# Output weights scaled by the gate, summed and split beside attention, and read back from DRAM by the output stage

## The chip, the cores and the metric

One NeuronCore of a Trainium2 chip. It has five engines with a queue of instructions each: TensorE (PE, matmuls, with a queue PEld for loading its stationary operand), VectorE (DVE), ScalarE (ACT), GpSimd (POOL) and SyncE (SP). Here SP does nothing but issue DMAs; ACT issues some too. DMAs move data between DRAM and SBUF, the on-chip memory; matmuls write to PSUM, eight banks of 128x512 float32. Every engine works through its queue in order and waits on semaphores. The metric is device time in microseconds (us) of one execution, the median of several runs.

## The reference, cut to what matters

One layer of a hybrid backbone over 2048 latent tokens of width 1024 (and 256 context tokens). One input projection feeds two token mixers: a gated DeltaNet, which gives `ya` (2048x512), and windowed attention, which gives `yb` (2048x512). Then

```python
def _merge(ya, yb, ga, gb, w_proj_a, w_proj_b, w_out):
    y = jax.nn.sigmoid(ga) * (ya @ w_proj_a) + jax.nn.sigmoid(gb) * (yb @ w_proj_b)
    return y @ w_out
...
x = x + gate[:, None] * _merge(ya, yb, ga, gb, w_proj_a, w_proj_b, w_out)
```

`gate` is a row of 1024 numbers that depends on the conditioning alone; `w_out` is 1024x1024. So the last stage is `x + gate * (y @ w_out)`, and the gate scales columns of `w_out`.

## The kernel before

Float32 products are made of reduced-precision ones: each operand is split into a high half (a cast, on ACT or POOL) and a low half (operand minus high half, on DVE or POOL), and a product is three matmuls per 128 rows of depth: high x high, high x low, low x high.

The parts that stand near the change, in order:

- **Attention** (`attention`, L943): 32 units, one for each of 16 blocks of 128 tokens and 2 key/value heads, in the token groups 1, 2, 0, 3 of 512 tokens. A unit's scores are made two units ahead (L978 masks, takes the minimum and reads PSUM; L980 exponentials; L988 scales on POOL), then `weighted` transposes them on PE, splits them (L1004 ACT, L1006 DVE) and multiplies by the values; L1014 on POOL multiplies by a gate and L1015 stores `yb`.
- **Gates** (`gates`, L892) fill PE between the units: columns 15 to 23 of the gate projections. Their weights are split at L243 and L244.
- **Projection** (`project`, L1280): for each token group, eight slices m of 128 channels of y, each the sum of two products, each scaled by a gate column from DRAM (L1304, L1309). For the groups 1, 2 and 0 they fill PE between attention's later units; group 3 comes after attention. y is stored to the scratch tensors `ysp` (L1310). The last two sums of group 3 are made late, within the output stage (`late_sum`, L1313). The projection's pool `proj` is opened at L1338, and its first loads of raw weights are at L1341.
- **Outputs** (from L1369): y is cut into 8 units of 256 tokens, each a 2x2 of quarters A11, A12, A21, A22 (128 tokens by 512 channels); `w_out` into quarters B11 to B22 of 512x512. Strassen's method in Winograd's form gives seven products per unit instead of eight: P1 = A11 B11, P2 = A12 B21, P3 = S4 B22, P7 = S3 T3, P6 = S2 T2, P5 = S1 T1, P4 = A22 T4, where S1 to S4 are sums of quarters of y (functions `s1` to `s4`), and T1 to T4 sums of quarters of `w_out`. One product is 12 matmuls of 128x512 (`product`, L1533 to L1541). `seq` is their order: for units 0 and 1 by turns, then unit by unit. `his(k)` casts the high half of product k's y operand on ACT five products ahead, `los(k)` makes the low half four products ahead (DVE, for P4 POOL). `outputs(k)` collects the finished product: sums of products in `held`, multiplication by the gate (`gbc`, the gate row on all partitions), addition of x (L1492) and the store (L1493), which also asks for the x tile four outputs on.

In the output stage the weight work is done on the spot: `load_w` brings the raw quarters on ACT's DMA queue, behind the last split of y for group 3; high halves are cast at L1438 to L1447, L1570, L1580 and L1585, low halves made in `split_lo` (L1411) on DVE and, for B22 and T3, on POOL; the sums T3, T2, T1, T4 are made in place at L1444, L1446, L1578 and L1583, between the products.

**What sets the order.** A planner (the tile framework) orders each engine's instructions by their place in the program and its own estimate of times: an instruction that is ready goes ahead of later ones, and later ones fill what is idle. `issue_after(i)` queues instructions behind i on its engine. Within `manual_schedule` the named engines keep the written order; in the output stage these are DVE, ACT, POOL and PE. SP's order is the planner's. SBUF is handed out in stacks from two sides; a tile that takes the bytes of an earlier one waits until that one was used for the last time.

Of the kernel before, what the change touches and what calls it, by code (L numbers as in the profile page):

```python
# [11 lines left out]
ALU = mybir.AluOpType  # L12
# [28 lines left out]
def _hybrid(ctx, tc, nc, V, S, G, T, ins, out, dbg, upto):  # L41
# [67 lines left out]
    ysp = many("ysp", 4, [128, KT, 512])  # L109
# [833 lines left out]
    def attention(pool, big, blocks, cc):  # L943
# [336 lines left out]
    def project(pool, wp, gi, yy=None, first=-99, late=()):  # L1280
# [3 lines left out]
        for m in range(KT):  # L1284
# [25 lines left out]
            dma(ysp[gi][:, m], us[0])  # L1310
        return left

    def late_sum(gi, m, us):  # L1313
        def run():
# [8 lines left out]
            dma(ysp[gi][:, m], ts[0])  # L1323
# [11 lines left out]
    attention(al, ar, [4 * gi + j for gi in (1, 2, 0, 3) for j in range(4)], att_consts(al))  # L1335
    gates(list(range(BESIDE, 22)), (1, 0))
# [37 lines left out]
    with tc.tile_pool(name="p4h", bufs=1, side="right", reuse_waits="tile") as hr, \  # L1374
# [9 lines left out]
        home = {"B11": er, "B21": er, "B22": el, "B12": el}  # L1384

        B = {nm: po.tile([128, 4, 512], F32, name=nm, tag=nm) for nm, po in home.items()}
        hi = {nm: BH(po, nm + "h") for nm, po in home.items()}
        hi["T3"] = hi["B12"]
        lo = {"B11": BH(er, "B11l")}
        A, Y = {}, {}  # L1390

        def load_w(nm):
            i, j = int(nm[1]) - 1, int(nm[2]) - 1
            adma(B[nm], ins["w_out"][0, i * 512:i * 512 + 512, j * 512:j * 512 + 512].rearrange("(k p) c -> p k c", p=128))

        def load_quad(u, nm):
            gi, o = units[u]
            if nm == "A2":
                t = p4.tile([128, 8, 128], F32, name="yA2", tag=f"yA2{u % 2}")
                adma(t, ysp[gi][:, :, o + 128:o + 256])  # L1400
                Y[u, "A21"], Y[u, "A22"] = t[:, 0:4], t[:, 4:8]
                return
            c = int(nm[2]) - 1
            po = {(0, "A11"): el, (0, "A12"): er, (1, "A11"): er}.get((u % 2, nm), p4)
# [3 lines left out]
        def split_lo(nm, eng, src=None, place=None):  # L1408
            if place:
                lo[nm] = home[place].tile([128, 4, 512], F32R, name=nm + "l", tag=place)  # L1410
            eng.tensor_tensor(lo[nm], B[src or nm], f32(hi[nm]), op=ALU.subtract)  # L1411
# [14 lines left out]

        with tc.high_priority(tc.cur_priority - p_last), \
                tc.manual_schedule(engines={EN.DVE, EN.Activation, EN.Pool}):
            with tc.issue_after(last["yh", 3].ins):
                load_w("B11")  # L1430
                load_quad(0, "A11")
                load_quad(1, "A11")
                load_w("B22")
                load_w("B12")
                load_w("B21")
                load_quad(0, "A12")
            with tc.issue_after(last["yh", 3].ins), tc.issue_after(last["yl", 3].ins):
                S.copy(hi["B11"], B["B11"])  # L1438
                split_lo("B11", V)
                for k in range(2):  # L1440
                    his(k)
                    los(k)
                S.copy(hi["B22"], B["B22"])
                V.tensor_tensor(B["B12"], B["B22"], B["B12"], op=ALU.subtract)  # L1444
                S.copy(hi["B21"], B["B21"])
                V.tensor_tensor(B["B11"], B["B12"], B["B11"], op=ALU.add)  # L1446
                S.copy(hi["T3"], B["B12"])  # L1447


        lo["B21"] = BH(hr, "B21l")  # L1450
        for k in range(2, NP):
            pair(k)
        for nm in ("B22", "T3"):
            lo[nm] = BH(hr, nm + "l")
        for nm in ("T2", "T1", "T4"):
            hi[nm] = BH(hr, nm + "h")
# [206 lines left out]
```

## Time and profile before

| | us |
|---|---|
| three runs, median (lowest, highest) | 1975.54 (1973.47, 1983.3) |
| the profiled execution: time / span | 1977.22 / 1975.5 |
| PE, DVE, ACT, POOL busy | 1902.6, 1512.4, 815.6, 701.3 |
| attention's first and last score (L978) | 1339.3, 1724.6 |
| first and last matmul of the outputs start | 1801.2, 1967.5 |

In the profile's rows L12 is line 12 of the kernel. A row of a timeline gives start, duration, engine, line, operation, output<-input, count, and in brackets how long the engine had stood idle and what released it. A row of waits gives who waited for whom: us in total, times, longest. A row of groups gives line, operation, count, then busy us in total and mean ns of one, then the idle time before them. PEclk, or the granted clock, is the share of full speed at which PE was allowed to run.

### The profile page before, as it was taken

The numbers are of one execution on the slowest core, as the hardware profiler recorded it, in microseconds if no ns is written. First come the engines' busy times: TensorE is split into PE (matmuls) and PEld (weight loads), VectorE is DVE, ScalarE is ACT, GpSimd is POOL, SyncE is SP. The second block draws the span as 40 slices with busy tenths as digits, with TensorE's granted clock in tenths as the row PEclk, the third lists the DMA queues.
The fourth block names the chain that finished last, engine by engine and source line by source line (L and its number), as shares of the span: only waits on it lengthen the run. The fifth ranks groups of instructions, "written<-read, shape, count | busy, mean of one in ns | idle before, by whom it ended". The sixth has DMA issues, their size and how long they took to land. (4 is left out here: it accounts for less than half of the span.)

```text
span 1975.5 us, 32093 instructions
## 1 busy us (share of the span) xinstructions
PE 1902.6 (96%) x10931; PEld 1596.3 (81%) x10931; DVE 1512.4 (77%) x2873; ACT 815.6 (41%) x2011; POOL 701.3 (35%) x772
## 2 busy tenths in 40 slices
PE   6899999989999899999999999999999999999998
PEld 3888888788998787887888888888878887877786
DVE  7888766678776899999778776535787868757888
ACT  6865545544443322211122233324765646532321
POOL 2652111235543201104222334323555443422675
PEclk9999999999999999999999999999999999999999
DMA  7453226765546633537887777765455645355453
GB/s 267 161 154 93 87 89 161 190 166 166 152 146 169 178 108 115 151 96 208 230 251 219 224 227 228 197 182 188 136 182 178 195 150 173 113 190 175 144 171 134
DMA packets 387640, 333.13 MB, mean 169 GB/s; under 512 B 83928, under 2 KB 307472, under 8 KB 386836
## 3 DMA queue, kind: packets, MB, share of 16 engines
q1 hardware_dynamic: 352132, 288.58, 50.4%
q10 hardware_dynamic: 35344, 42.49, 6.2%
q8 instruction: 87, 1.43, 0.3%
q14 instruction: 77, 0.63, 0.1%
HBM read 220.28 MB, written 109.13 MB: 167 GB/s over the span
## 5 line engine op out<-in xcount | busy, mean ns | idle before, releaser
L586 PE MATMUL rps<-hh,wh 128*128 128x512 f32 x768 | 308.5, 402 | 6.5 <-DVE rt L880 5.4
L588 PE MATMUL rps<-hh,wl 128*128 128x512 f32 x768 | 307.7, 401 | 0.2 <-DVE wl L244 0.2
L587 PE MATMUL rps<-hl,wh 128*128 128x512 f32 x768 | 306.3, 399 | 0.0
L625 DVE SCALAR_TENSOR_TENSOR cacc<-y,cw,cacc 128x512 f32<-128x512 f32 (+1 forms) x224 | 163.5, 752 | 23.3 <-ACT cacc L623 21.0
L586 PEld LDWEIGHTS rps<-hh,wh 128*128 128x128 f32 x768 | 144.9, 189 | 41.8 <-DVE rt L880 6.3
L588 PE MATMUL lps<-hh,wl 128*128 128x512 f32 (+1 forms) x448 | 171.6, 383 | 1.7 <-DVE wl L244 1.7
L586 PE MATMUL lps<-hh,wh 128*128 128x512 f32 (+1 forms) x448 | 172.0, 384 | 0.8 <-POOL wh L243 0.6
L588 PEld LDWEIGHTS rps<-hh,wl 128*128 128x128 f32 x768 | 144.8, 188 | 32.6 <-DVE wl L244 0.3
L587 PEld LDWEIGHTS rps<-hl,wh 128*128 128x128 f32 x768 | 144.8, 189 | 32.5
L587 PE MATMUL lps<-hl,wh 128*128 128x512 f32 (+1 forms) x448 | 171.0, 382 | 0.0
L1006 DVE TENSOR_TENSOR pl<-pt,ph 128x512 fp32r<-128x512 f32 x156 | 105.6, 686 | 42.3 <-ACT ph L1004 41.4
L1004 ACT CAST ph<-pt 128x512 fp32r<-128x512 f32 x156 | 90.8, 585 | 107.8 <-PE pt L1002 72.8
L878 ACT ACTIVATE rt<-rps 128x512 f32<-128x512 f32 x96 | 57.2, 596 | 181.5 <-PE rps L588 157.9
L978 DVE CUSTOM_DVE_ANT_0 pr<-sc,band,sk 128x640 f32<-128x640 f32 (+1 forms) x128 | 106.7, 862 | 19.8 <-PE sc L974 12.1
L988 POOL TENSOR_SCALAR pr<-pr,sm 128x640 f32<-128x640 f32 (+1 forms) x128 | 101.4, 813 | 54.7 <-DVE sm L986 39.9
L809 DVE TENSOR_TENSOR btmp<-N 128x62 f32<-128x62 f32 (+30 forms) x124 | 117.4, 946 | 3.1
L811 DVE TENSOR_TENSOR N<-N,btmp 128x62 f32<-128x62 f32 (+30 forms) x124 | 116.1, 936 | 3.0
L980 ACT ACTIVATE pr<-pr,sm 128x640 f32<-128x640 f32 (+1 forms) x128 | 104.1, 815 | 24.1 <-DVE sm L978 24.1
L1293 PE MATMUL pps<-yh,wph 128*128 128x512 f32 x256 | 105.7, 415 | 2.4 <-DVE tb L1304 2.1
L244 DVE TENSOR_TENSOR wl<-wr,wh 128x512 fp32r<-128x512 f32 x120 | 91.6, 775 | 20.2 <-POOL wh L243 17.9
L243 POOL TENSOR_SCALAR wh<-wr 128x512 fp32r<-128x512 f32 x72 | 49.5, 700 | 156.4 <-PE lps L587 85.2
L1295 PE MATMUL pps<-yh,wpl 128*128 128x512 f32 x256 | 101.6, 398 | 0.9 <-POOL wpl L1255 0.9
(382 smaller groups left out, 5028.2 us busy)
## 6 DMA issues: line engine op xcount, KB each, us to landing
wr<-in_w_in_dram SPq DMA_DIRECT2D x120, 256.0 KB
kw<-Ksp SPq DMA_DIRECT2D x28, 384.0 KB
x<-vsp SPq DMA_DIRECT2D x36, 256.0 KB
k<-ksp SPq DMA_DIRECT2D x34, 256.0 KB
kT<-kTsp SPq DMA_DIRECT2D x34, 256.0 KB
wm<-in_w_mod_dram SPq DMA_DIRECT2D x16, 512.0 KB
xt<-in_x_dram SPq DMA_DIRECT2D x16, 512.0 KB
dtl<-Dsp SPq DMA_DIRECT2D x32, 256.0 KB
```

The costliest lines, as they stand in the source:

```text
L586: T.matmul(ps, lhsT=wh[:, k], rhs=xh[:, k], start=k == 0, stop=False)
L587: T.matmul(ps, lhsT=wh[:, k], rhs=xl[:, k], start=False, stop=False)
L588: T.matmul(ps, lhsT=wl[:, k], rhs=xh[:, k], start=False, stop=k == kt - 1)
L625: V.scalar_tensor_tensor(a, y[:, t:t + n], cw[:, m, t:t + 1], a, op0=ALU.mult, op1=ALU.add)
L809: V.tensor_tensor(tv, A[:, m + 1:, m].unsqueeze(2).to_broadcast([h1 + n, r, m]), A[:, m, 0:m].unsqueeze(1).to_broadcast([h1 + n, r, m]), o ...
L811: V.tensor_tensor(A[:, m + 1:, 0:m], A[:, m + 1:, 0:m], tv, op=ALU.add)
L978: V.tensor_tensor_reduce(s_, ps[:, o:768], band[:, b0:b0 + W + 256], -0.125, sk[:, 1, hd:hd + 1], ALU.add, ALU.min, sm[:, h, 1:2])
L980: S.activation(s_, s_, AF.Exp, scale=-1.0, bias=sm[:, h, 1:2], accum_out=sm[:, h, 2:3])
L988: G.tensor_scalar(p[:, h, :W + 256], p[:, h, :W + 256], sm[:, h, 3:4], 1.0, op0=ALU.mult, op1=ALU.mult)
L1006: V.tensor_tensor(pl, pt, f32(ph), op=ALU.subtract)
L1293: T.matmul(ps, lhsT=wh[:, k, ms], rhs=hs[k], start=k == 0, stop=False)
L1295: T.matmul(ps, lhsT=wl[:, k, ms], rhs=hs[k], start=False, stop=k == 3)
```

## The change

1. A generator `out_weights` runs beside attention: one step after each unit, 25 steps. For each of four slices of 128 rows it loads that slice of the four quarters of `w_out`, multiplies them by the gate row (`gbc`, POOL), makes T3, T2, T1 and T4 in place (POOL), casts the high half of each of the seven (ACT), makes the low half (DVE), and stores both to the scratch tensors `wsp` in DRAM. Its pool `wout` is closed behind attention and the gates; the pool `proj` opens at the same place of the left stack.
2. In the output stage `load_w` loads finished high and low halves: B11, B21, B22, T3 on ACT's queue with the first quarters of y, T2, T1 and T4 on SP's queue, between the first x tiles. All casts, splits and sums of weights are gone from there, and s3 and s2 of units 0 and 1 stand ahead of the products.
3. As the weights hold the gate, outputs need no multiplication: `gather` adds a product, or a sum in `held`, straight into the x tile; `store` adds the last product to it from PSUM and stores it. P1 is added on POOL, P3 on DVE, the three sums behind P6 on POOL (for the last unit on DVE). Eight x tiles instead of four are kept.
4. `ysp` is laid out as [4, 128, 8, 128], one block for each 128 tokens, so that a quarter of y is contiguous per partition (2 KB, or 4 KB for A21 and A22 together) and a store is cut into runs of 512 bytes.

```diff
-    ysp = many("ysp", 4, [128, KT, 512])
+    ysp = many("ysp", 4, [4, 128, KT, 128])
+    wsp = {nm: [dscr(f"w{nm}{x}", [128, 4, 512]) for x in "hl"] for nm in ("B11", "B21", "B22", "T3", "T2", "T1", "T4")}
...
+    def out_weights(pool):
+        gbc = pool.tile([128, D], F32, name="gbc")
+        dma(gbc, gsp.to_broadcast([128, D]))
+        b = {}
+        def load(k):
+            for nm in ("B22", "B12", "B11", "B21"):
+                i, j = int(nm[1]) - 1, int(nm[2]) - 1
+                b[nm] = pool.tile([128, 512], F32, name=nm)
+                dma(b[nm], ins["w_out"][0, i * 512 + k * 128:i * 512 + k * 128 + 128, j * 512:j * 512 + 512])
+        def gated(nm):
+            j = int(nm[2]) - 1
+            G.tensor_tensor(b[nm], b[nm], gbc[:, j * 512:j * 512 + 512], op=ALU.mult)
+        def put(k, nm, t):
+            h = pool.tile([128, 512], F32R, name="woh", bufs=2)
+            l = pool.tile([128, 512], F32R, name="wol", bufs=2)
+            S.copy(h, t)
+            V.tensor_tensor(l, t, f32(h), op=ALU.subtract)
+            for dst, p in zip(wsp[nm], (h, l)):
+                dma(dst[:, k], f32(p))
+        load(0)
+        yield
+        for k in range(4):
+            gated("B22")
+            gated("B12")
+            yield
+            put(k, "B22", b["B22"])
+            G.tensor_tensor(b["B12"], b["B22"], b["B12"], op=ALU.subtract)
+            gated("B11")
+            yield
+            put(k, "T3", b["B12"])
+            put(k, "B11", b["B11"])
+            G.tensor_tensor(b["B11"], b["B12"], b["B11"], op=ALU.add)
+            yield
+            gated("B21")
+            put(k, "T2", b["B11"])
+            G.tensor_tensor(b["B22"], b["B22"], b["B11"], op=ALU.subtract)
+            yield
+            put(k, "T1", b["B22"])
+            put(k, "B21", b["B21"])
+            G.tensor_tensor(b["B21"], b["B21"], b["B11"], op=ALU.subtract)
+            yield
+            put(k, "T4", b["B21"])
+            if k < 3:
+                load(k + 1)
+            yield
...
             weighted(n, kv, qs[n], pr.pop(i))
+            next(beside, None)
...
-            dma(ysp[gi][:, m], us[0])
+            dma(ysp[gi][:, :, m].rearrange("o p c -> p o c"), us[0].rearrange("p (o c) -> p o c", c=128))
...
-        def load_w(nm):
-            i, j = int(nm[1]) - 1, int(nm[2]) - 1
-            adma(B[nm], ins["w_out"][0, i * 512:i * 512 + 512, j * 512:j * 512 + 512].rearrange("(k p) c -> p k c", p=128))
+        def load_w(nm, queue=adma):
+            for t, x, src in zip((hi, lo), "hl", wsp[nm]):
+                t[nm] = BH(home.get(nm, hr), nm + x)
+                queue(f32(t[nm]), src)
...
-            adma(Y[u, nm], ysp[gi][:, c * 4:c * 4 + 4, o:o + 128])
+            adma(Y[u, nm], ysp[gi][o // 128][:, c * 4:c * 4 + 4])
...
-        def store(u, q, t, eng):
-            xr, dst, gate, j = X.pop((u, q))
-            eng.tensor_tensor(t, t, gate, op=ALU.mult)
-            (V if u == 7 else G).tensor_tensor(xr, t, xr, op=ALU.add)
+        def gather(eng, u, q, t):
+            xr = X[u, q][0]
+            eng.tensor_tensor(xr, t, xr, op=ALU.add)
+        def store(u, q, ps):
+            gather(V, u, q, ps)
+            xr, dst, j = X[u, q]
             dma(dst, xr)
-            load_x(j + 4)
+            load_x(j + 8)
...
             if nm == "P1":
                 S.copy(held[u][:, 0], ps)
+                gather(G, u, "00", held[u][:, 0])
             elif nm == "P2":
-                og = ev.tile([128, 512], F32, name="og", tag="rt")
-                V.tensor_tensor(og, ps, held[u][:, 0], op=ALU.add)
...
+                store(u, "00", ps)
+            elif nm == "P3":
+                gather(V, u, "01", ps)
             elif nm == "P6":
                 V.tensor_tensor(held[u][:, 0], ps, held[u][:, 0], op=ALU.add)
                 V.tensor_tensor(held[u][:, 1], R[u, "P7"], held[u][:, 0], op=ALU.add)
+                gather(gp, u, "11", held[u][:, 1])
+                gather(gp, u, "01", held[u][:, 0])
+                gather(gp, u, "10", held[u][:, 1])
             elif nm == "P5":
-                h2 = wq.tile([128, 2, 512], F32, name="hold2", tag="wl")
-                V.tensor_tensor(h2[:, 0], ps, held[u][:, 0], op=ALU.add)
-                V.tensor_tensor(h2[:, 1], ps, held[u][:, 1], op=ALU.add)
-                V.tensor_tensor(h2[:, 0], R[u, "P3"], h2[:, 0], op=ALU.add)
...
+                store(u, "11", ps)
+                store(u, "01", ps)
             elif nm == "P4":
-                V.tensor_tensor(held[u][:, 1], ps, held[u][:, 1], op=ALU.add)
-                store(u, "10", held[u][:, 1], gp)
+                store(u, "10", ps)
...
+            for j in range(2):
+                load_x(j)
+            load_w("T2", dma)
+            for j in range(2, 8):
+                load_x(j)
+            for nm in ("T1", "T4"):
+                load_w(nm, dma)
```

More of the change, by code (lines that the diff above doesn't have):

```diff
@@ L941, in att_consts, with attention @@
         return kc, vc, sk, band
-    def attention(pool, big, blocks, cc):
+    def out_weights(pool):
[43 more added lines that the diff above has]
+            yield
+    def attention(pool, big, blocks, cc, beside=()):
         kc, vc, sk, band = cc
@@ L1334, in _hybrid @@
     ar = ar_.__enter__()
-    attention(al, ar, [4 * gi + j for gi in (1, 2, 0, 3) for j in range(4)], att_consts(al))
-    gates(list(range(BESIDE, 22)), (1, 0))
+    with tc.tile_pool(name="wout", bufs=1, reuse_waits="tile") as wo:
+        attention(al, ar, [4 * gi + j for gi in (1, 2, 0, 3) for j in range(4)], att_consts(al), out_weights(wo))
+        gates(list(range(BESIDE, 22)), (1, 0))
     wp, last = {}, {}
@@ L1425, in los @@
             (G if nm == "P4" else V).tensor_tensor(A[k][1], Y[u, OPS[nm][0]], f32(A[k][0]), op=ALU.subtract)
[L1427 to L1456, printed above, removed]
         def s3(u, eng):
@@ L1473, in s1 @@
             Y[u, "S1"] = Y[u, "A11"]
-        R, held, early = {}, {}, {}
+        with tc.high_priority(tc.cur_priority - p_last), \
+                tc.manual_schedule(engines={EN.DVE, EN.Activation, EN.Pool}):
+            with tc.issue_after(last["yh", 3].ins):
+                load_w("B11")
+                load_quad(0, "A11")
+                load_quad(1, "A11")
+                load_w("B21")
+                for q in ((0, "A12"), (0, "A2"), (1, "A12"), (1, "A2")):
+                    load_quad(*q)
+                load_w("B22")
+                load_w("T3")
+            with tc.issue_after(last["yh", 3].ins), tc.issue_after(last["yl", 3].ins):
+                for k in range(2):
+                    his(k)
+                    los(k)
+                s3(0, V)
+                s2(0, V)
+                s3(1, V)
+                s2(1, V)
+        for k in range(2, NP):
+            pair(k)
+        R, held = {}, {}
         outs = [(u, q) for u, nm in seq for q in {"P2": ["00"], "P5": ["11", "01"], "P4": ["10"]}.get(nm, [])]
@@ L1540, in product @@
                 T.matmul(ps, lhsT=h[:, j], rhs=wl[:, j], start=False, stop=False)
-                end = T.matmul(ps, lhsT=l[:, j], rhs=wh[:, j], start=False, stop=j == 3)
-            return end
+                T.matmul(ps, lhsT=l[:, j], rhs=wh[:, j], start=False, stop=j == 3)
         with tc.manual_schedule(engines={EN.DVE, EN.Activation, EN.Pool, EN.PE}):
@@ L1546, in _hybrid @@
                 next(j)
-            split_lo("B21", V)
+            for j in range(2):
[5 more added lines that the diff above has]
+                load_w(nm, dma)
             his(2)
-            for q in ((1, "A12"), (0, "A2"), (1, "A2")):
-                load_quad(*q)
-            gbc = p4.tile([128, D], F32, name="gbc")
             los(2)
-            next(sums67[0])
+            s4(0)
             his(3)
             los(3)
-            split_lo("B22", G)
-            split_lo("T3", G, "B12")
-            s3(0, V)
-            s2(0, V)
-            s4(0)
+            next(sums67[0])
             his(4)
+            s4(1)
             for k in range(len(seq) + 1):
@@ L1592, in _hybrid @@
                     load_quad(2, "A2")
-                    for u in range(2):
-                        store(u, "00", *early[u])
                 elif k == 11:
@@ L1610, in _hybrid @@
                 if k < len(seq):
-                    end = product(k)
-                if k == 3:
-                    with tc.issue_after(end.ins):
-                        dma(gbc, gsp.to_broadcast([128, D]))
-                        for j in range(4):
-                            load_x(j)
+                    product(k)
                 if k:
```

54 lines of the change are left out of this document (9 added, 45 removed).

## The prediction

> **What bounds the kernel now.** I read the page's busy times first, then a table of stretches of the span, then the stalls of TensorE in the last stage, then the order of time around them.
>
> ```profile
> PE 1902.6 (96%) x10931; PEld 1596.3 (81%) x10931; DVE 1512.4 (77%) x2873; ACT 815.6 (41%) x2011; POOL 701.3 (35%) x772
> ```
>
> TensorE (PE) is the bound: at most 1975.5 - 1902.6 = 72.9 us of the span are not its matmuls. The change removes no matmul, so it can only win or lose idle PE time. Where that lies (columns: stretch, length, then PE, PEld, DVE, ACT and POOL busy with counts, granted clock, DMA share, GB/s):
>
> ```profile
> 1339.00:1350.00 11.00, 11.00 (x51) 9.07 (x50) 4.97 (x14) 4.17 (x10) 1.25 (x2) 1.00 0.83 269
> 1350.00:1452.00 102.00, 100.94 (x563) 84.97 (x562) 77.54 (x175) 69.87 (x154) 48.72 (x55) 1.00 0.46 142
> 1452.00:1500.00 48.00, 44.70 (x241) 36.68 (x240) 37.48 (x72) 30.80 (x65) 33.33 (x30) 1.00 0.63 198
> 1875.00:1968.00 93.00, 92.88 (x402) 74.94 (x400) 79.59 (x89) 19.29 (x35) 65.44 (x41) 1.00 0.48 156
> ```
>
> Attention begins at 1339. Its first eight units (to 1452) run with PE full, filled by gate columns; then the projections fill it. From 1875 to 1968 the outputs run with PE full too: one product of 12 matmuls takes 12 x 93/402 = 2.78 us there. The idle time of the output stage lies before, in six stretches, and behind it:
>
> ```profile
> 1805.00:1810.00 5.00, 2.38 (x11) 1.63 (x9) 5.00 (x1) 0.00 (x0) 4.87 (x2) 1.00 1.05 349
> 1810.00:1815.00 5.00, 4.52 (x13) 3.57 (x14) 4.65 (x8) 0.62 (x1) 0.00 (x0) 0.66 0.74 209
> 1830.00:1835.00 5.00, 3.44 (x15) 2.51 (x14) 5.00 (x5) 2.82 (x4) 0.00 (x0) 1.00 0.00 0
> 1850.00:1855.00 5.00, 3.98 (x18) 2.94 (x18) 5.00 (x8) 2.35 (x5) 3.68 (x3) 1.00 0.85 243
> 1855.00:1860.00 5.00, 3.39 (x15) 2.47 (x14) 5.00 (x7) 0.00 (x0) 3.68 (x4) 1.00 0.80 259
> 1865.00:1870.00 5.00, 4.28 (x19) 3.16 (x18) 2.59 (x3) 0.02 (x1) 5.00 (x4) 1.00 0.38 125
> ```
>
> The idle PE time adds up to 2.62 + 0.48 + 1.56 + 1.02 + 1.61 + 0.72 = 8.0 us. In 1810 to 1815 the clock was 0.66, which stretched 4.52 busy us by about 4.52 x 0.34 = 1.5 us. What ends these stalls, and why the first is so long (waits of the stage, then DVE and POOL in order of time):
>
> ```profile
> PE P L1541 <- DVE al L1425: 7.3, 4, 3.1
> PE P L1541 <- POOL al L1425: 0.7, 1, 0.7
> PE pps L1293 <- DVE tb L1304: 2.1, 1, 2.1
> ...
> 1798.45 2.29 DVE L1411 TENSOR_TENSOR B21l<-B,B21h 128x2048 fp32r<-128x2048 f32 x1 [1.99 <-PE pps L1294]
> 1800.66 9.76 DVE L1425 TENSOR_TENSOR al<-yA,ah 128x512 fp32r<-128x512 f32 x1
> ...
> 1798.71 6.59 POOL L1411 TENSOR_TENSOR B22l<-B,B22h 128x2048 fp32r<-128x2048 f32 x1 [41.01 <-PE pps L1295]
> 1805.26 4.61 POOL L1411 TENSOR_TENSOR T3l<-B,B12h 128x2048 fp32r<-128x2048 f32 x1
> ```
>
> The first two rows say that all eight us are waits for low halves. The one of 9.76 us ends at 1810.4, just behind POOL's two weight splits (1809.9). So a DVE operation with two SBUF operands stands still while POOL works on SBUF.
>
> **The change, part by part.**
>
> *Output stage, weights.* It loses, on DVE, four sums and five splits of 128x2048 (2.29 us each, 20.6 us), on POOL the two splits of 11.2 us, and on ACT seven big casts; the last of them stand between PE's products. The stall at 1805 loses its cause. So do those at 1830, where DVE is full (5.00 of 5.00) with big sums ahead of the low half, and at 1850 to 1860, where DVE is full with the gate multiplications.
>
> *Output stage, outputs.* Per unit DVE had nine operations on outputs (one for P2, two for P6, three plus two gate multiplications for P5, one for P4) and gets seven; POOL had two multiplications and four additions and gets four. Two new waits: the store of 00 on DVE waits for POOL's addition of P1 into x, and the additions of P5 wait for POOL's three of P6. Queued behind them on DVE are low halves that PE needs three to four products later (8 to 11 us), against three POOL additions of 1.68 us (L1492 below); I put that at 0, at most one POOL operation per unit. I take 7 of the 8 us and the clock's 1.5: **-8.5**; ends 0 (other DVE waits take their place) and -9.5 (all).
>
> *Tail.* After the last matmul:
>
> ```profile
> 1967.48 0.40 PE L1541 MATMUL P<-T4h,al 128*128 128x512 f32 x1
> ...
> 1971.81 0.69 DVE L1527 TENSOR_TENSOR xr<-hold,xr 128x512 f32<-128x512 f32 x1
> 1972.53 0.33 SPq L1528 DMA_DIRECT2D out_dram<-xr  x1
> ```
>
> PE ends at 1967.88, DVE's backlog at 1972.50, the span at 1975.5: 7.6 us. Afterwards one addition from PSUM is left (0.69), 0.1 of hand-over, and the same store (1975.5 - 1972.53 = 2.97): 3.8 us. P5's two additions are done by then, as P4 takes 2.78. **-3.8**; ends -2 (a store queued behind P5's two) and -4.
>
> *Weights come late.* Seven pairs, 14 x 1.05 MB = 14.7 MB, are read where 4.2 MB were. B11, B21, B22, T3 and the first halves of y go on ACT's queue, 10.5 MB, from the time of the first row. T2, T1 and T4 lie where the projection's weights were and can't start before those are read for the last time:
>
> ```profile
> 1764.12 0.39 ACTq L1394 DMA_DIRECT2D B<-in_w_out_dram  x1
> 1798.38 0.62 ACT L1421 CAST ah<-yA 128x512 fp32r<-128x512 f32 x1 [14.20 <-PE pps L1294]
> ...
> L1539 PE MATMUL P<-B11h,ah x32: 387/393/398, 1801.2 to 1950.4; 128*128 128x512 f32 x32
> ...
> DMA packets 3809, 5.25 MB, mean 328 GB/s; under 512 B 122, under 2 KB 1629, under 8 KB 3808
> ```
>
> The second row shows such a start today. From 1798.6 there follow 1.05 MB for the late sums, T2, eight x tiles, T1 and T4, 9.4 MB: at the 349 GB/s of the stretch from 1805, 27 us, so T4 at 1826. The outputs start at 1801.2, and it is needed 12 products later, 1801 + 12 x 2.78 = 1834. The margin of 8 us pays for 3 MB of leftover, new y quarters and stores; the last row is the rate of 1764 to 1780, which also holds the wait for its first bytes. I take **+1.5**, a mid of 0 and the late case below, nearer to 0; the first low half may also wait for the projection's last matmul, 0 to 1 us, within this.
>
> *y quarters.* Stores of y go in runs of 512 B (2 KB before), 32 of 256 KB; loads in runs of 2 or 4 KB (512 B before). The rows give no time by run length. PE waited 2.1 us for the projection's sums in the whole trace (third row of the waits), so I take 0, ends -1 and +2.
>
> *Attention.* Added there: 16 loads and 28 x 2 stores of 256 KB, 32 POOL operations, 28 casts and 28 subtractions of 128x512. Prices (groups of 1339 to 1452, then of the output stage):
>
> ```profile
> L982 DVE TENSOR_TENSOR es<-sm,sk 128x4 f32<-128x4 f32 x11 | 4.1, 371 | 0.0
> L1255 POOL TENSOR_TENSOR wpl<-wpr,wph 128x512 fp32r<-128x512 f32 x4 | 5.1, 1289 | 2.4 <-ACT wph L1254 2.4
> L1274 ACT CAST yh<-yr 128x512 fp32r<-128x512 f32 x4 | 2.3, 612 | 0.0
> L1275 DVE TENSOR_TENSOR yl<-yr,yh 128x512 fp32r<-128x512 f32 x2 | 1.3, 689 | 0.0
> ...
> L1492 POOL TENSOR_TENSOR xr<-hold,xr 128x512 f32<-128x512 f32 x21 | 35.1, 1685 | 27.9 <-DVE hold L1491 21.1 <-DMA xr<-in_x_dram 4.9 <-DMA yA<-ysp 1.3
> L1425 DVE TENSOR_TENSOR al<-yA,ah 128x512 fp32r<-128x512 f32 x40 | 51.9, 1311 | 6.3 <-ACT ah L1421 5.6 <-PE P L1541 0.8
> ```
>
> ACT: 28 x 0.61 = 17 us, against 39 idle from 1339 to 1452; nothing. POOL: 32 x 1.29 = 41 us alone, 54 at the 1.685 beside DVE, against 63 idle. One round of a k is a chain of eight POOL operations, 10 to 13 us, plus its loads and attention's own POOL work, some 25 us by estimate, so the four rounds take about 100 us from 1336 on, units 0 to 8. DVE: it is idle 6.0 + 24.5 = 30.5 us up to 1452. Alone the 28 subtractions are 28 x 0.69 = 19.3 us and fit: 0. Beside a busy POOL I price them as the low halves of today's outputs, 28 x 1.31 = 36.7, and attention's two small sums per unit (L982 already varies about 0.37) at half a us more, 10 units, 10 us. That is 46.7, 16.2 more than is idle. The planner gives attention's units precedence over later steps, so the surplus runs on into 1452 to 1500, where DVE has 10.5 us idle: **+6**. Ends -1 (the planner orders all anew, which can gain a little) and +24 (below). If the cover of idle DVE were gone, all 46.7 would be on the path.
>
> [...]
>
> DMA: 4.2 + 14.7 + 0.5 = 19.4 MB in some 100 us, 194 GB/s on top of 142, within the 349 seen. SP issues in order, so a store of a part that waits for ACT or DVE holds up attention's next loads of keys, queries and gates behind it; those run two units (about 20 us) ahead. Next to this, the projection's first raw weights lie in the same bytes and are loaded today at
>
> ```profile
> 1335.62 2.53 SPq L1341 DMA_DIRECT2D wpr<-in_w_proj_a_dram  x4
> ...
> 1453.37 1.07 SPq L1273 DMA_DIRECT2D yr<-ybsp  x2
> ```
>
> 1335.6, but nothing uses them before y of the first group is loaded, at 1453. They may come 110 us later at no cost; beyond that each us costs a part of one.
>
> *Sum*, against the profiled execution's 1977.2 us (span 1975.5): 1977.2 - 8.5 - 3.8 + 1.5 + 6 = 1972.4. That execution lies 1.7 above the median of the runs, 1975.5, so I predict **1971**.
>
> **The rivals.**
>
> 1. *Attention has the room.* PE idled 1.1 us in 1350 to 1452 and DVE has 30.5 us to spare; if the subtractions fall where POOL rests, attention pays 0, and the loads nothing. 1977.2 - 8.5 - 3.8 - 1.7 = 1963. Against it: DVE's idle time there waits for PE and ACT, so it comes in short pieces.
>
> 2. *DVE becomes the bound of attention: slower.* One mechanism: subtractions and small sums wait for POOL in the units before 1452, where PE has no other work to take. If every subtraction waits out one POOL operation, 28 x (0.69 + 1.29) = 55 us, plus 10 for the small sums, less 30.5 and 10.5: +24, so 1977.2 - 8.5 - 3.8 + 1.5 + 24 - 1.7 = 1989. From +11 on the change gains nothing. For it: the 9.76 us; against it: POOL is half idle there, and the low halves of 1.31 us show the mean wait under a POOL as busy.
>
> 3. *The late weights take the stall's place.* At 230 GB/s (the stretches from 1810 and 1850 show 209 and 243) the 9.4 MB last 41 us, T4 is at 1840, 5 us late, and with the 3 MB of others up to 18. At +9 instead of +1.5: 1979. Against it: big runs ran at 328 and more.
>
> 4. *It does not do what it says:* the 8 us are waits that find another cause (low halves behind PSUM additions), the tail alone is won, and attention costs 6: 1977.2 - 3.8 + 1.5 + 6 - 1.7 = 1979.
>
> **How the numbers follow.** Forecast 0.49 (own range 1966 to 1978), rival 1 0.24, rival 2 0.14, rivals 3 and 4 0.13 together. About 0.5%, 9.9 us, is what a measurement of this kernel can tell from no change, so faster means below 1965.7 and slower above 1985.4. Faster: rival 1 and 0.05 of the forecast, 0.29. Slower: 0.12 of rival 2 and 0.01 of rival 3, 0.13. Same: 0.58. The range reaches from rival 1 with -1 and all 8 us (1961) to the near half of rival 2, 1986.
>
> **What the profile after would show.** DVE's low halves at the stage's start last about 0.7 us, and PE's waits for them fall from 8.0 us below 2; no PE wait there names a DMA of T1 or T4. From the last matmul to the end some 4 us. In attention DVE is over 90% busy for the first eight units and PE idles some 6 us more there than before. The low-half subtractions of the new weights average 1.0 to 1.4 us. The forecast is wrong if PE idles over 15 us more before 1500, if a T weight lands after its product is due, or if the stalls between 1800 and 1870 persist.

## The result, and the profile after

The changed kernel is slower by 1.3%: 2003.99 us (median; 2000.96 to 2006.95) beside 1977.27 us for the kernel before (1973.47 to 1983.3), a ratio of 1.0133 with a 95% interval of 1.0117 to 1.0149, about 26 us. One execution of the kernel before took 9533.77 us and is left out of these numbers. The forecast was 1971, with 1986 as the upper end. The profiled execution took 2006.95 us (span 2005.2), 29.7 us of span more than the one before.

First line of the page, and TensorE's waits from 1800 to the end, in the changed kernel:

```profile
PE 1915.5 (96%) x10931; PEld 1609.7 (80%) x10931; DVE 1475.1 (74%) x2872; ACT 819.4 (41%) x2032; POOL 710.4 (35%) x789
```

```profile
PE P L1566 <- ACT ah L1467: 21.6, 1, 21.6
```

One wait is left in the output stage where six stretches had eight us, but it is 21.6 us long. Stretches of the changed kernel (columns as in the prediction), and then one of the kernel before:

```profile
1350.00:1500.00 150.00, 134.57 (x704) 109.86 (x703) 130.06 (x248) 102.75 (x219) 112.58 (x102) 0.98 0.81 265
...
1820.00:1825.00 5.00, 4.04 (x18) 2.91 (x16) 0.00 (x0) 0.00 (x0) 0.00 (x0) 1.00 0.83 261
1825.00:1845.00 20.00, 0.00 (x0) 0.00 (x0) 0.00 (x0) 0.00 (x0) 0.00 (x0) 0.53 1.00 382
1845.00:1850.00 5.00, 4.32 (x10) 3.36 (x11) 4.22 (x7) 2.48 (x5) 0.00 (x0) 0.50 1.03 420
1850.00:1900.00 50.00, 50.00 (x220) 41.01 (x220) 36.72 (x50) 13.07 (x23) 22.69 (x15) 1.00 0.73 257
```

```profile
1350.00:1500.00 150.00, 145.63 (x801) 121.66 (x800) 115.02 (x246) 100.67 (x217) 82.05 (x85) 1.00 0.51 160
```

From these the 29.7 us can be laid out. The projection ends at 1824.1 where the outputs started at 1801.2: **+22.9**. Then the stall: **+21.6**. From the first product (1845.7) to the last matmul (2001.6) it takes 155.9 us where it took 166.7: **-10.8**, though the clock was 0.50 in the first five of them. And the tail is 3.6 us where it was 7.6: **-4.0**. The end in order of time (PE, then DVE; the span ends at 2005.2):

```profile
2001.24 0.39 PE L1568 MATMUL P<-T4h,al 128*128 128x512 f32 x1
...
1999.45 1.28 DVE L1528 TENSOR_TENSOR xr<-P,xr 128x512 f32<-128x512 f32 x2
2001.67 0.69 DVE L1528 TENSOR_TENSOR xr<-P,xr 128x512 f32<-128x512 f32 x1 [0.93 <-PE P L1568]
```

So the two gains came, 14.8 us. Two costs ate them and more.

**Cost one, attention.** In the 150 us from 1350 TensorE did 704 matmuls instead of 801; at 150/801 us each the missing 97 are some 18 us (an estimate, as their sizes are mixed). PE idled 15.4 us there, 11 more than before, and the clock was 0.98. The other 5 of the 22.9 are no work of the change: at 1339, before attention, this execution was 25 matmuls behind the other one (7841 against 7866, summed over four stretches to there; the loss is that of the first 100 us, 473 against 499 at a granted clock of 0.90 against 0.97), and executions of the kernels below lie anywhere from 7839 to 7877. DVE's groups from 1339 to 1470, then TensorE's largest wait there (in total):

```profile
L964 DVE TENSOR_TENSOR wol<-B,woh 128x512 fp32r<-128x512 f32 x28 | 26.1, 944 | 11.5 <-ACT woh L963 6.9 <-DMA wT2l<-wol 2.4 <-DMA wT3l<-wol 1.8
L1036 DVE TENSOR_TENSOR es<-es,sm 128x4 f32<-128x4 f32 x10 | 5.4, 536 | 0.9 <-ACT es L1035 0.9
```

```profile
PE av L1061 <- DVE pl L1058: 8.1, 8, 2.2
```

The small sums of the second row took 536 ns each, where they took 296 over the same stretch of the kernel before (L984).

**Cost two, the stall.** ACT's instructions in order of time (ACTq is the issue of a DMA on its queue; left out are the issues of A12, A2, B22 and T3h):

```profile
1789.13 0.33 ACTq L1445 DMA_DIRECT2D B11h<-wB11h  x1
1789.49 0.45 ACTq L1445 DMA_DIRECT2D B11l<-wB11l  x1
1810.57 7.02 ACTq L1457 DMA_DIRECT2D yA<-ysp  x2
1821.14 0.33 ACTq L1445 DMA_DIRECT2D B21h<-wB21h  x1
1828.14 0.33 ACTq L1445 DMA_DIRECT2D B21l<-wB21l  x1
...
1844.64 0.33 ACTq L1445 DMA_DIRECT2D T3l<-wT3l  x1
1845.01 2.18 ACT L1467 CAST ah<-yA 128x512 fp32r<-128x512 f32 x4 [55.27 <-DMA xr<-in_x_dram]
```

The first cast that TensorE needs stands behind fourteen issues, and these aren't issued one after the other: 21 us lie between B11l and the first quarter of y. The cast's row names an x tile in brackets, but on its own queue the cast stands behind T3l's issue at 1844.64. The kernel's instruction listing tells why:

```
1598 L1457 DMA yA11 <- ysp1   [waits DMAHW2]
1599 L1457 DMA yA11 <- ysp1   [waits DMAHW5]
1600 L1445 DMA B21h <- wB21h  [waits DMAHW7]
...
1610 L1467 CAST ah <- yA11    [waits DMAHW2]
```

The framework gives the transfers of SP's and ACT's queues eight completion counters in turn, in the order that the planner foresaw, and an issue waits for the earlier transfer of its counter. SP's waits show the same: its x tiles wait for weights with which they share no byte.

```profile
SPq L1523 <- DMA T2l<-wT2l: 4.7, 1, 4.7
SPq L1523 <- DMA T2h<-wT2h: 2.9, 1, 2.9
```

In time ACT's loads lie among SP's gate columns and stores of the last projection, which wait for TensorE, and SP's x tiles (1824.1), which wait for the projection's end. By the same listing both quarters of A11 and both halves of B21 wait for gate columns of that projection, and the first A12 for an x tile. Once the issues came free, bytes set the pace: from 1825 to 1845 the DMA share was 1.00.

### The profile page after: what moved, and what is told of

It is laid out like the page before. It is cut to its first block, busy times and chain, and to the rows that moved or that the text cites. A ratio compares the mean times of both kernels' runs of the same rounds, so it can differ in the third digit from the quotient of the medians.

```text
span 2005.2 us, 32306 instructions
## 1 busy us (share of the span) xinstructions
PE 1915.5 (96%) x10931; PEld 1609.7 (80%) x10931; DVE 1475.1 (74%) x2872; ACT 819.4 (41%) x2032; POOL 710.4 (35%) x789
## 5 line engine op out<-in xcount | busy, mean ns | idle before, releaser
L626 DVE SCALAR_TENSOR_TENSOR cacc<-y,cw,cacc 128x512 f32<-128x512 f32 (+1 forms) x224 | 164.7, 757 | 21.6 <-ACT cacc L624 19.2
```

What stands on the lines that cost most here:

```text
L626: V.scalar_tensor_tensor(a, y[:, t:t + n], cw[:, m, t:t + 1], a, op0=ALU.mult, op1=ALU.add)
```

## The experiments

Theory: (A) the stall comes from these issue waits; (B) attention pays because the new operations stand in the in-order queues of ACT, DVE and POOL. Rivals: the stall comes from the bytes; attention's price is small or one engine's. The kernel before ran beside each group at 1977.1 to 1977.9 us; differences in us are the ratio times 1977.5.

### Each part alone

```diff
 e1: the kernel before
+    attention(..., out_weights(wo))        # nothing reads its stores
```


> The kernel before with the weights' work beside attention and nothing else: the finished halves are stored to DRAM and not read, the output stage is the old one. Theory: of the 23 us by which the changed kernel's projection ends later, 11 are PE idle in attention's first units and some 5 a lower granted clock there, so this kernel takes 12 to 18 us more than the kernel before (1992 to 1998 beside 1980), with PE idle in 1350 to 1450 at about 12 us. My forecast's price was 6 us: 1986. Rival: the delay was mostly a slow clock in the first 100 us of that one execution and has nothing to do with attention: 1980 to 1983.

```diff
 e2: the changed kernel
-    attention(..., out_weights(wo))
+    attention(...)
-                queue(f32(t[nm]), src)
+                queue(f32(t[nm]) ..., Qsp[i:i + 2] ...)
```


> The changed kernel without the work beside attention: the seven high and low halves are loaded, in the same order on the same queues, from DRAM that the kernel wrote long before (the queries of attention), so the product is not that of the output weights and the gate is left out. Theory: the 21.6 us stall at the start of the outputs comes from the order of loads on ACT's queue and stays, 15 to 22 us; the rest of the stage is some 11 us shorter and the tail 4: 1980 + 20 - 15 = 1985, range 1980 to 1990. Rival: the stall comes from what stands beside attention (late projections, stores that the loads wait for) and goes with it: 1964 to 1968.

```diff
 e4: the kernel before
-    ysp = many("ysp", 4, [128, KT, 512])
+    ysp = many("ysp", 4, [4, 128, KT, 128])   # with its stores and loads
```


> The kernel before with the new layout of y alone (stores in runs of 512 bytes, quarters loaded in runs of 2 and 4 KB). Theory: no change, -1 to +2 us: 1979 to 1982. Rival: the stores in short runs hold up DMA at the end of the projection, +5 us and more, with PE waits for loads of gate columns or quarters of y.

Measured: e1 1997.41 us, ratio 1.0100 (1.0075 to 1.0125), **+20**. e2 1986.39, ratio 1.0041 (1.0027 to 1.0056), **+8**, with its stall in place (`PE P L1516 <- ACT ah L1417` 21.2 us). e4 1978.37, ratio 1.0001 (0.9983 to 1.0019), nothing. The sum, 20 + 8 + 0 = 28, is near the 26 us of the whole: the two costs are separate, and the stall doesn't come from what stands beside attention. e1's stretch shows the loss of the changed kernel almost to the matmul:

```profile
1350.00:1500.00 150.00, 134.17 (x703) 108.95 (x704) 131.50 (x250) 103.52 (x222) 112.18 (x101) 0.99 0.81 266
```

### What the stall waits for

```diff
 e3: the changed kernel, ACT's order
                 load_quad(1, "A11")
+                his(0), los(0), his(1), los(1)
                 load_w("B21")
```


> The changed kernel with the first two casts (ACT) ahead of the issues of B21, A12, A2, B22 and T3; the same loads, bytes and queues. Theory: PE's first product waits for a cast that stands behind fourteen load issues, each of which waits for an earlier transfer; with the casts ahead PE starts when the projection ends, and later waits for B21, B22 and T3 come to 6 to 10 us: 10 to 16 us less than the changed kernel, 1988 to 1994. Rival: the bytes are what is late, and PE waits the same 21 us in other places: 2000 to 2005.

Measured: 2008.42 us, ratio 1.0158 (1.0130 to 1.0187): nothing gained, as the rival said. ACT's casts, and the load that the third product needs:

```profile
1816.81 0.62 ACT L1467 CAST ah<-yA 128x512 fp32r<-128x512 f32 x1 [27.43 <-DMA ta<-gasp]
1819.25 0.62 ACT L1467 CAST ah<-yA 128x512 fp32r<-128x512 f32 x1 [1.82 <-DMA yA<-ysp]
...
1835.55 0.33 ACTq L1457 DMA_DIRECT2D yA<-ysp  x1
...
1850.38 1.14 ACT L1467 CAST ah<-yA 128x512 fp32r<-128x512 f32 x2 [30.50 <-DMA yA<-ysp]
```

The first two casts are now done before the projection ends, and the stall moves to the third product, 21.3 us. The order of casts and loads is not enough: the loads themselves go out late (A12 at 1835.55). Bytes or waits was the next question.

```diff
 e5: the changed kernel, half the bytes, each slice used twice
-                queue(f32(t[nm]), src)
+                queue(f32(t[nm][:, :2]), src[:, :2])
 e6: the changed kernel, seven loads
-    wsp = {nm: [dscr(f"w{nm}{x}", [128, 4, 512]) for x in "hl"] ...
+    wsp = {nm: dscr(f"w{nm}", [128, 2, 4, 512]) ...
 e7: the changed kernel
-        def load_w(nm, queue=adma):
+        def load_w(nm, queue=G.dma_start):
```


> The changed kernel with the same fourteen weight loads in the same order, each of half the bytes (the halves hold two of four slices of depth, and the products use each slice twice, so the output is not the reference's); PE does the same matmuls. Theory, issue waits: ACT's loads wait for transfers of SP's queue until the projection ends, whatever their size; only the waits behind 1824, when DMA is full, get shorter. The stall falls from 21.6 to about 12: 1993, range 1989 to 1999. Rival, bytes alone: the loads use the time from 1789 on and the stall goes below 4: 1982 to 1986. Second rival, waits alone: it stays at 20: 2002.

> The changed kernel with the high and low half of a weight in one scratch tensor and one load: the same bytes, seven weight loads where there were fourteen, ten issues on ACT ahead of the first cast. Theory, issue waits: fewer issues wait for transfers of the other queue, the stall falls from 21.6 to 12 to 16: 1994 to 1999. Rival, bytes alone: no change, 2002 to 2006.

> The changed kernel with the loads of B11, B21, B22 and T3 on POOL's queue, where their issues do not wait for transfers of SP's queue and POOL has nothing to do; ACT keeps six issues of y quarters ahead of the first cast, T2, T1 and T4 stay on SP. Theory, issue waits: the weights land before the projection ends, the first cast follows the y quarters, PE's stall falls from 21.6 to 0 to 6: 1981 to 1988. Rival, bytes alone: the stall stays above 15: 1998 to 2004. Second rival: POOL's way of starting transfers is slow, and PE waits for B21 or B22 by name.

Measured: half the bytes 1998.77 us (ratio 1.0116, 1.0100 to 1.0133), stall 17.3. All bytes in half the loads 1997.60 (1.0112, 1.0088 to 1.0137), stall 17.0. So halving the bytes does no more than halving the issues, some 4 us of the 21.6 each: bytes alone are out, and my 12 us for e5 was too hopeful. With the weights on POOL's queue 2003.28 (1.0138, 1.0117 to 1.0158), a miss of the theory's 1981 to 1988. TensorE's waits in it, then the order of time of POOL's and ACT's rows:

```profile
PE pps L1346 <- DVE tb L1357: 11.2, 1, 11.2
PE P L1566 <- ACT ah L1467: 10.4, 1, 10.4
```

```profile
1780.70 1.24 ACT L1327 CAST yh<-yr 128x512 fp32r<-128x512 f32 x2 [12.35 <-DMA yr<-yasp]
1787.20 0.53 POOL L1445 DMA_DIRECT2D T3l<-wT3l  x1
...
1826.59 8.48 ACTq L1457 DMA_DIRECT2D yA<-ysp  x3
```

The weights were all issued by 1787.7, the last four at 0.53 to 0.59 us each (0.33 to 0.45 on ACT in the changed kernel), but the quarters of y, still on ACT, only from 1826.6 on: half of the stall stays with no weight ahead of it. The other half became a stall in the projection: the gate column's operation (`tb`) stands on DVE behind a low half, whose cast waited 12.35 us for an input of the projection (first row). That input was loaded beside the weights, with the DMA share at 1.01 from 1770 to 1780. So bytes do count where loads go out together.

```diff
 e9: e6, with the last group's project() and the loads of late_sum()
-                dma(t, tsp[gi][m])
+                G.dma_start(t, tsp[gi][m])
-            dma(ysp[gi] ..., us[0] ...)
+            G.dma_start(ysp[gi] ..., us[0] ...)
 e10: e9, with the start of the outputs
-                load_x(j)
+                load_x(j, G.dma_start)
-                load_w(nm, dma)
+                load_w(nm, G.dma_start)
```


> The changed kernel with one load for both halves of a weight (seven loads), and with the small transfers of the last projection (its gate columns and its stores of y) on POOL's queue, so that the loads of ACT's queue have no late transfer of SP's queue ahead of them. Theory, issue waits: B11, the y quarters and B21 are issued within some 10 us of the first, DMA is full 20 us earlier, the first cast follows by 1815, and PE's stall falls from 21.6 (17.0 with the seven loads alone) below 6: 1982 to 1988. Rival, bytes: the weights crowd out the projection's gate columns, and PE waits for those by name, as with the loads on POOL's queue, 1990 to 1998. Second rival: the waits are on other transfers than these, the stall stays at 15 to 17: 1996 to 2000.

> The changed kernel with seven weight loads, and with every transfer of SP's queue that stands in time between ACT's loads moved to POOL's queue: the last projection's gate columns and stores of y, the first eight x tiles, and T2, T1 and T4. Theory, issue waits: an issue on ACT or SP waits for an earlier transfer of either queue; in the run before, A21/A22 of the first unit was issued at 1828.8, some 4 us behind SP's first x tiles (1824.3), which wait for the last matmul of the projection. With these gone ACT's ten loads are issued from 1790 to 1805, and PE's stall at the start falls from 14.9 to below 3: 1982 to 1986, ratio 1.003 to 1.005. Rival, bytes: the same bytes still come late, PE waits 10 us or more, by the name of a cast, a weight or a gate column: 1992 to 1998.

Measured: e9 1997.40 us, ratio 1.0097 (1.0068 to 1.0125), stall 14.9: the second rival, other transfers. ACT's issues in order of time, then SP's of the x tiles:

```profile
1791.07 1.20 ACTq L1445 DMA_DIRECT2D B<-wB  x1
1798.57 0.33 ACTq L1458 DMA_DIRECT2D yA<-ysp  x1
1828.83 0.33 ACTq L1452 DMA_DIRECT2D yA<-ysp  x1
...
1824.31 0.81 SPq L1524 DMA_DIRECT2D xr<-in_x_dram  x2
```

Five loads now go out by 1799, but the sixth, A21 and A22, follows SP's x tiles by 4.5 us. With these moved as well (e10) 1985.76 us, ratio 1.0046 (1.0032 to 1.0060): the time that the theory gave, with a stall of 4.9 us where I had expected less than 3. TensorE's wait in the stage, then ACT's first and last load:

```profile
PE P L1569 <- DVE al L1472: 4.9, 1, 4.9
```

```profile
1784.53 0.33 ACTq L1445 DMA_DIRECT2D B<-wB  x1
...
1794.08 0.33 ACTq L1445 DMA_DIRECT2D T<-wT  x1
```

Ten loads with the same bytes as in e6 are issued within 10 us, and of the stall 4.9 us are left, a low half that stands on DVE behind late gate columns. That shows (A): it took the removal of both kinds of SP's transfers; the order gained nothing, and bytes and number some 4 us each.

### The stage without its two costs

```diff
 e11: e10
-    attention(..., out_weights(wo))
+    attention(...)                         # loads read Qsp, as in e2
```


> The changed kernel's output stage alone: nothing beside attention (the finished halves are read from DRAM that the queries were written to, so the product is not that of the output weights and the gate is left out), seven weight loads, and no transfer of SP's queue between ACT's loads. Theory: the stage gains 11 us (8 of stalls, 1.5 of clock and the late sums' place) and the tail 4, less 3 to 5 us for a low half that waits at the start behind gate columns, as in the run before: 1977.5 - 10 = 1967, range 1964 to 1971. Rival: the stage's gain was the other side of the stall at its start, which gave DVE time to work ahead; without the stall the waits for low halves come back: 1974 and above.

Measured: 1970.54 us, ratio 0.9959 (0.9943 to 0.9975), **-8**. Its waits in the stage:

```profile
PE P L1517 <- DMA T<-Qsp: 3.6, 1, 3.6
PE P L1519 <- DVE al L1422: 3.1, 1, 3.1
```

The gain of the stage and tail is real and doesn't need the stall. With attention's 20 it makes +12, and e10 measured +9 (6 to 12). One weight was late by name, 3.6 us: T4, whose load was issued last on POOL's queue, at 1822.29, behind the projection's small transfers, the x tiles, T2 and T1. That is rival 3's case, which the changed kernel itself didn't show.

### What attention pays for

All are e1 with a part left out; the price is that over the kernel before, the matmuls those in 1350 to 1500.

```diff
 a1: no low halves
-            V.tensor_tensor(l, t, f32(h), op=ALU.subtract)
 a2: 14 of 56 stores
+            if k == 3:
                 for dst, p in zip(wsp[nm], (h, l)): dma(...)
 a4: no work on POOL
-            G.tensor_tensor(b[nm], b[nm], gbc[...], op=ALU.mult)     # and the four sums
 a6: a1 and a4 together
 a5: loads and place alone
```


> The kernel before with the weights' work beside attention (nothing reads its results), without the low-half subtractions on DVE; the high half is stored twice, so stores, casts and POOL's work stay. Theory: DVE's 27 us of subtractions, and the 11 us in which they stand at the head of its queue waiting for casts and stores, are what attention pays; without them the price falls from 20 us to 2 to 7: 1980 to 1985. Rival: the price is that of transfers and of SP's order (56 stores, DMA share 0.8): it stays at 14 us or more, 1991 and above. Second rival: POOL's work that delays its scaling of the scores: 1988 to 1992.

> The kernel before with the weights' work beside attention, with 14 of its 56 stores (the last slice's only, so the scratch tensors are not filled and nothing reads them). Theory, SP's order and transfers: stores that wait for casts and subtractions stand ahead of attention's loads, and take the buffers of the next casts; without them the price falls from 20 us to 12 or less: below 1990. Rival, the engines' own queues: attention's casts, subtractions and scalings stand behind the new operations on ACT, DVE and POOL; the price stays at 16 to 20: 1993 to 1998.

> The kernel before with the weights' work beside attention, without its 32 operations on POOL (no gate multiplication and no sums, so the raw quarters are cast, split and stored). Theory, POOL: its operations hold up the scaling of the scores and stretch DVE's small sums (245 to 577 ns) and subtractions (690 to 970 ns); without them the price falls from 20 us to 6 to 10: 1984 to 1988. Rival, ACT, DVE and transfers: it stays at 15 or more, 1992 and above.

> The kernel before with the weights' work beside attention, without POOL's work and without the low halves: 16 loads, 28 casts on ACT and 56 stores are left. Theory, shares add up: 20 us less 4 for the subtractions and 7 for POOL leaves 9 for casts waiting at the head of ACT's queue: 1985 to 1988. Rival, DVE beside POOL: each of the two alone was enough to hold up attention, and without both the price is 0 to 4: 1977 to 1981.

> The kernel before with nothing beside attention but the sixteen loads of the weights' slices and the gate row (each touched by a copy of eight columns on POOL) and the place that they take. Theory: the price is that of operations in the engines' queues, and this one costs 0 to 3 us: 1977 to 1980. Rival: the place and the loads delay the projection's raw weights, or the planner orders all anew, 6 us and more: 1983 and above.

| kernel | median us | ratio (95%) | price us | matmuls |
|---|---|---|---|---|
| e1, all | 1997.41 | 1.0100 (1.0075 to 1.0125) | 20 | 703 |
| a2, few stores | 1999.67 | 1.0114 (1.0081 to 1.0147) | 23 | 678 |
| a1, no low halves | 1993.01 | 1.0081 (1.0056 to 1.0105) | 16 | 736 |
| a4, no POOL work | 1990.45 | 1.0064 (1.0043 to 1.0085) | 13 | 742 |
| a6, neither | 1986.67 | 1.0044 (1.0032 to 1.0056) | 9 | 748 |
| a5, loads alone | 1979.62 | 1.0011 (0.9999 to 1.0023) | 2 | 797 |

The stretch of a5, then that of a6 and TensorE's largest wait in it:

```profile
1350.00:1500.00 150.00, 145.03 (x797) 121.40 (x796) 115.36 (x248) 102.23 (x221) 86.70 (x108) 1.00 0.58 184
```

```profile
1350.00:1500.00 150.00, 139.68 (x748) 116.50 (x748) 104.34 (x229) 105.87 (x227) 74.70 (x78) 0.98 0.81 269
```

```profile
PE av L1054 <- ACT ph L1050: 7.4, 5, 3.0
```

Place and loads cost nothing that can be told (2 us, with an interval that holds 0). Fewer stores gain nothing, though the DMA share falls from 0.81 to 0.57. Each engine's share is small (e1's interval overlaps those of a1 and a4), but the shares add up, and a6 lies where their sum put it: 4 for the subtractions, 7 for POOL's work and the waits for it, and 7 from a5 to a6 for casts and stores together. No run has the casts without the stores; since fewer stores gained nothing in a2, I put the 7 down to the casts. In a6 ACT has only 28 casts of 0.6 us more, and is 70% busy, yet TensorE waits 7.4 us for attention's own casts: a new cast at the head of ACT's queue that waits for its input or its buffer holds up the ones behind it. That fits (B), but it isn't shown for each wait. The theories of a1 (DVE alone is the price) and a2 (the stores are) were wrong.

### A version without the detour

Three versions of the kernel before, in which POOL multiplies the raw weights by the gate as they arrive and outputs gather in x as in the change, were meant to beat both.

```diff
 c2, c6, c8: the kernel before, start of the output stage
+                adma(gbc, gsp.to_broadcast([128, D]))     # c6: behind B11; c8: POOL's queue, x tiles too
+                for nm in ("B11", "B22", "B12", "B21"):   # c6: in the order of need
+                    G.tensor_tensor(B[nm][:, k], B[nm][:, k], gbc[...], op=ALU.mult)
```


> A version without the detour: the kernel before, where POOL multiplies the raw weights by the gate at their arrival in the output stage (16 operations of 128x512, some 21 us, in POOL's idle 41 us ahead of that stage), and outputs gather in the x tiles as in the changed kernel. Theory: nothing is added to attention or to the loads; it keeps the shorter tail (4 us) and the 2.6 us of stalls at 1850 to 1860, where DVE was full with gate multiplications, and loses 0 to 2 at the start: 1971 to 1974 beside 1977.5, ratio 0.997. Rival: the gated weights come late to DVE's and ACT's splits, and PE waits at the start of the outputs: 1980 and above.

> The version without the detour again, with the gate row loaded behind B11, and the quarters loaded, gated, cast and split in the order of need (B11, B21, B22, B12). Theory: loads go out at 1764 as in the kernel before, POOL's 21 us of gating end at about 1806, PE's stalls at the start are as before or 3 us more, those of 1850 to 1860 and half of the tail are gone: 1971 to 1977, ratio 0.997 to 1.0. Rival: DVE and POOL hold each other up there, and low halves of weights come late: 1980 and above.

> The version without the detour, with the gate row and the first four x tiles loaded on POOL's queue, so that ACT's loads are those of the kernel before. Theory: ACT's loads go out from 1764 on as before, POOL's gating ends by 1800 to 1806, and of the gain the shorter tail and the stalls at 1850 to 1860 stay, less 0 to 3 us at the start: 1971 to 1976. Rival: gating on POOL holds up DVE's big splits and sums (2.29 us each) and comes late for B21, whose high half is due at the third product: 1980 and above.

Measured: 2005.47 (ratio 1.0139, 1.0112 to 1.0165), 2006.54 (1.0143, 1.0121 to 1.0165) and 1997.02 (1.0108, 1.0083 to 1.0133). In c2, where the gate row goes ahead of B11, the first load was issued at 1788.8. In c6 it goes behind B11, and the quarters and x tiles are loaded in another order (order of time):

```profile
1771.12 0.39 ACTq L1394 DMA_DIRECT2D B<-in_w_out_dram  x1
1791.50 0.33 ACTq L1432 DMA_DIRECT2D gbc<-gsp  x1
1798.60 4.26 ACTq L1406 DMA_DIRECT2D yA<-ysp  x2
```

The gate row went out 20 us behind B11 and everything behind it later still; the kernel before issued all seven loads from 1764 to 1770. TensorE's longest wait in c6, 20.6 us, is for a low half that stands on DVE behind sums that waited for POOL's gating. In c8, where ACT has the loads of the kernel before and no other, the quarters of y were late again (1781.65), so the extra load alone isn't the cause. By the programs' listings the first issue behind B11 waits in both for a gate column of the last projection, and in the kernel before for none; which part of the edits moved the turns wasn't isolated. POOL's gating in c8, over at 1815, met DVE's splits: one of 128x2048 on DVE took 11.32 us instead of 2.29, beside two on POOL (DVE, then POOL):

```profile
1817.01 11.32 DVE L1411 TENSOR_TENSOR B21l<-B,B21h 128x2048 fp32r<-128x2048 f32 x1 [4.31 <-ACT B21h L1451]
...
1817.20 4.53 POOL L1411 TENSOR_TENSOR B22l<-B,B22h 128x2048 fp32r<-128x2048 f32 x1
1821.69 4.48 POOL L1411 TENSOR_TENSOR T3l<-B,B12h 128x2048 fp32r<-128x2048 f32 x1
```

No version here beats the kernel before. DVE's waits for POOL are real: besides these 11.32 us, in the output stage of the kernel before (1800 to 1975) a DVE operation of 128x512 with two SBUF operands took 0.68 us while POOL was idle and mostly 1.2 to 1.8 us beside it, one with a PSUM operand 0.68 us either way. But in attention POOL's work, with the waits for it, was 7 us of the 20 and not the main price.

## Why the prediction was wrong

- **Stage, weights and outputs (-8.5, with the two new waits at 0): right in mechanism.** The six stalls are gone; low halves of y take 0.68 us (the median) and TensorE is full from 1850 on. The profile gives -10.8 from first product to last matmul, past my end of -9.5, but there the stall gave DVE time to work ahead. Without it, in e11, stage and tail together give -8, against a forecast of -12.3, with 6.7 us of other waits in it, 3.1 of them for a low half.
- **Tail (-3.8): right**, -4.0, with 3.6 us left.
- **Weights come late (+1.5, ends 0 and +9): the term that failed first.** It measured +21.6, and some 2 us of half clock behind it (4.32 busy us at 0.50). I let a transfer start when its bytes were free and then counted bytes at 349 GB/s. Bytes did not start the stall: the DMA share was only 0.54 in the changed kernel from 1750 to 1800, and in e10 the same bytes left 4.9 us of it. What was late were the issues, and the casts behind them; only then did the bytes meet, and DMA ran full through the stall (share 1.00, 382 GB/s). Rival 3 looked at T2, T1 and T4, which were late for nobody there. The row for it stood in my own prediction: ACT's first load at 1764.12 and its casts in one queue. I counted the bytes that the fourteen issues move, and not what each waits for.
- **y quarters (0): right**, -3 to +4 us (e4).
- **Attention (+6, ends -1 and +24): the second term that failed.** It measured +20 (15 to 25), rival 2's size but not rival 2. Of its steps, the subtraction's price was too high (944 ns measured, 1310 assumed: 26 us, not 37), and DVE was 87% busy from 1350 to 1500 (130.06 of 150), not over 90. But DVE also stood 11.5 us behind waits at the head of its queue, which I didn't count, POOL's work cost 7 where I gave it idle time, and casts and stores cost some 7 where I wrote "nothing" for the casts. Idle time covers a new operation only if it's ready when that time comes; in an in-order queue it also delays what stands behind it (argued from the waits above, not shown for each).
- **The signs named.** PE's extra idle before 1500 was 11 us, inside the 15 that I set as the limit, while 97 matmuls were missing: idle time alone understates such a loss. No T weight was late in the changed kernel. The third sign, stalls from 1800 to 1870, was the one that fired.
- The **chances** followed from the two bad terms: the rival on the other side (0.14) needed attention's +24 alone, and I had no case in which both costs came together.

Open: some 4 of the 22.9 us aren't placed by what the rows give directly (5 of the start, 11 idle, 3 of clock: 150 x 0.02). Whether weights made in another phase would pay wasn't tried.

## What to carry to other kernels

A load is an instruction in an in-order queue, and here also a turn on a counter that it shares with the other queue: before loads are added to a queue that computes too, list the issues ahead of each cast and ask what each waits for, not only how many bytes pass. Work put "beside" other work pays on every engine that it touches, a little each (here some 4, 7 and 7 us), even where no engine is full. A forecast that sums small terms should hold one case in which two of them fail at once.

## What the runs showed that was not expected

- Edits at the start of a stage can move the turns on the counters: in c6 and c8 the second issue on ACT's queue came 20 and 21 us behind the first, where the kernel before has 0.5 us (1764.12 and 1764.63).
- One core moved up to 433 GB/s (e9, 1840 to 1845), well above the 349 on which I had counted, and the loads of the stall ran at 382 to 420 GB/s (the row is e9's):

```profile
1840.00:1845.00 5.00, 5.00 (x19) 4.08 (x18) 4.93 (x9) 1.35 (x3) 0.00 (x0) 0.79 1.05 433
```

- The stall cost more than its length: the granted clock was 0.50 in the 5 us around its end (10 matmuls in 4.32 busy us, where 1850 to 1900 has 22 per 5 us). From 1850 to 1855 the clock was 0.99 again.
- Single executions of these kernels differ by up to 38 matmuls at 1339 us of the span, before attention begins (some 8 us, at the 183 matmuls that the kernel before did in the 39 us to there), so a difference of two single profiles is worth less than that of the medians.
